# Copying a table of relative biases 128 times: out of SBUF, or from DRAM to DRAM

## The chip, the core and the metric

The kernel runs on one core of a Trainium2 chip. Its engines are TensorE (PE in the rows, its weight loads PEld), VectorE (DVE), ScalarE (ACT), GpSimd (POOL) and SyncE (SP). Here every transfer is issued by SP, in one queue, and carried by the core's 16 DMA engines. The metric is the device time of one execution in microseconds; before the change it is 3177.89 us, the median of three runs (3168.99, 3177.89 and 3178.84).

## The reference, cut to what matters

The reference is one inference step of a decoder layer, for 512 prompt tokens and 8 x 8 sample tokens that share all weights: a projection into four mixers (gated delta rule, a diagonal state space model S5, sliding-window attention with dilations, a gated linear recurrence), their product with `w_out`, cross attention, and a SwiGLU with a convolution. The change touches one input of the window attention, the T5 bias that each logit gets by its distance:

```python
for win, dil in DILATED:
    dist = jnp.arange(win // dil + 1, dtype=jnp.int32) * dil
    bias = rel_bias[t5_bucket(dist)].T.astype(jnp.float32)
    groups.append((dist, bias))
...
logits = jnp.einsum('bqhd,bqshd->bhqs', qi32, kg) * scale + bias[None, :, None, :]
```

`rel_bias` has 32 buckets by 8 heads. The kernel joins the three groups by a logarithm of how often a distance occurs, so that one table of 8 heads by 647 distances serves all of them.

## The kernel before, in words

All 576 tokens stay on chip, with features on partitions. A product with a weight matrix (`linear`, L132 on) takes the weights in blocks of 4 x 128 rows by 256 columns: `block` (L114 on) loads one of 512 KB into `raw` (L119, two buffers), ScalarE makes its upper part `hi` (L128, four instructions), VectorE its lower part `lo` (L129, four instructions), and TensorE does 48 matmuls (L151) with them into two PSUM tiles `acc`. A block's `raw` buffer is free for the block after next once its last `lo` is done, and after four blocks VectorE takes the sums out of `acc` (L1052 to L1054 in `conv4`), before TensorE may start on the next group.

A planner that simulates the engines writes the order of instructions for each engine, by priorities: weights first, then the work of the mixers, then the projections' matmuls as filling. It also shares out SBUF: a pool that is closed gives its place to a later one, and whoever first writes there waits for the last reader of what lay there. In `run`, the pool `st` of `swa_tables` is closed just before the pool `sm` of the S5 stage is opened on the same side.

`swa_tables` (L658 on) is the place of the change. It loads the one-hot table of buckets and the logarithms (`lm`, 8 partitions by 647), multiplies `rel` by the one-hots (L673) and adds the product to `lm` (L674). Then L675 writes `lm` to `rb` in DRAM, 8 heads by 128 copies by 647: each head's row 128 times. With the copies, a read whose partition step is 646 instead of 647 gives every query the table shifted by one place; `sample_new` (L891, L892, from 453 us of the profile on) and `swa_prompt` (L782, from 903 us on) read `rb` in this way.

Names of the rows that follow: `dn` is the delta rule's rows on their way to DRAM (L1251), `W` (L1736) and `u` (L1740) are what the S5 stage loads first into the pool `sm`, `hbg` (L1860) and `H` (L1763) are tiles of that pool which VectorE writes first, `hs` (L1766) and `rt` (L1751) are later loads of the stage, `ut` (L1742) is a copy of `u` that TensorE turns (L1745), and `old` (L813) are cached keys.

Of the kernel before, what the change touches and what calls it, by code (L numbers as in the profile page):

```python
# [7 lines left out]
F32 = mybir.dt.float32  # L8
# [4 lines left out]
PSUM = bass.MemoryType.PSUM  # L13
DRAM = bass.MemoryType.DRAM
NT = 576
EPS = 1e-6


class Net:
# [11 lines left out]
    @contextmanager  # L31
    def at(self, level, banks=None):
        """What is issued inside has this priority, and takes its PSUM banks in turn from these."""
        tc = self.tc
        saved, tc.cur_priority = tc.cur_priority, self.levels[level]
        old = self.banks
        self.banks = banks or old
        yield
        self.banks = old
        self.levels[level] = max(self.levels[level], tc.cur_priority)  # L40
        tc.cur_priority = saved
# [7 lines left out]
    def nt(self, n=NT, dtype=F32):  # L49
        """A row of all tokens, from a ring."""  # L50
        self.turn += 1
        return self.wo.tile([128, 604], dtype, name="nt", tag="m" + "hl"[self.turn % 2], bufs=6)[:, :n]

    def open(self):
        """What the first norm needs."""
        nc, cp, a = self.nc, self.cp, self.a
        self.ident = cp.tile([128, 128], F32, name="ident")
        self.gmix = cp.tile([128, 16], F32, name="gmix")
        with self.at("first", (3,)), self.tc.tile_pool(name="gp", bufs=1) as gp:
            nc.sync.dma_start(self.ident, a["c_ident"])  # L60
            g = gp.tile([16, 128], F32, name="g")
            nc.sync.dma_start(g, a["g_mix"][0].rearrange("(k p) -> k p", p=128))
            p = self.pm()
            nc.tensor.transpose(p[:, :16], g, self.ident[:16, :16])
            nc.scalar.copy(self.gmix, p[:, :16])

    def consts(self, vp):
        """Rows of 128 features each, turned into columns."""
# [30 lines left out]
    def rstd(self, pool, ss, n, scale, rows=128, eps=EPS, bufs=1):  # L99
        """1/sqrt(ss*scale + EPS) for ss [rows, n], with one Newton step."""  # L100
# [13 lines left out]
    def block(self, w, k0, nk, c0, ncol, gain=None):  # L114
        """nk row tiles by ncol columns of w, times the rows' gain if there is one, split into two parts of 12 bits."""
# [16 lines left out]
    def linear(self, xh, xl, w, c0, ncol, done, k0=0, nk=None, gain=None):  # L132
        """done(i, ps) gets each tile of 128 columns of x @ w as [128, 576]."""
# [24 lines left out]
    def project(self, c0, ncol, done):  # L158
        """Columns of the normed x @ w_in, but for 1/rms."""
        self.linear(self.xh, self.xl, self.a["w_in"][0], c0, ncol, done, gain=self.gmix)  # L160

    def mem_kv(self, mp, ahead):
        """Keys (turned) and values of the prompt's memory: out, and to DRAM for the cross attention."""
# [6 lines left out]
        for kb in range(0, 16, 2):  # L170
            if kb == 14:
                ahead()
            with self.at("drain"):
                # each row's scale waits for the products
# [47 lines left out]
    def first_x(self, fp, keep):  # L222
        """x turned, in two parts; 1/rms of each token, on every partition, joins the products."""
# [52 lines left out]
    def scaled(self, dst, ps, s=None):  # L276
        """A product's tile by the tokens' 1/rms."""
# [7 lines left out]
class Post(Net):  # L285
    def add_x(self, g=None, first=False):
        """What adds tiles of a product to x; after the last one x is scaled and split, and its squares summed."""
# [25 lines left out]
    def row_rstd(self):  # L313
        """1/rms of each token of xT, on every partition."""
# [28 lines left out]
    def sample_kT(self, cw, pair):  # L343
        """The cached memory's keys turned, two heads of each batch."""
# [11 lines left out]
    def cross(self, cw):  # L356
        """Two heads at a time; the product with w_mem_o takes the first two while the others are worked on."""
# [5 lines left out]
        def softmax(L, n):  # L363
            """rows of L [128, n, 256], in PSUM."""
# [31 lines left out]
        def sample(pair):  # L396
# [11 lines left out]
            # rows (j, b, t) in quarters; of a quarter's four batches each takes 128 columns  # L408
# [20 lines left out]
        def head(h, ps):  # L429
            q[h] = self.wo.tile([128, 604], F32, name="q", tag="ml", bufs=6)[:, :NT]  # L430
            nc.vector.tensor_tensor(q[h], ps, self.r, op=OP.mult)
            # block b of the mask's diagonal
# [27 lines left out]
    def ffn(self):  # L460
# [9 lines left out]
        with ExitStack() as c:  # L470
# [3 lines left out]
            with self.at("mix"):  # L474
                # rows (g, b, k): an eighth of the features each
# [15 lines left out]
            def states(ready):  # L491
                """These conv states, which are complete, out."""
# [9 lines left out]
            def conv(ft, ps, slot):  # L502
                """The taps of feature tile ft; its last raw rows go to the state."""
# [56 lines left out]
    def final(self, fh, fl, fw, fo):  # L560
        """The last part of the product with w_down by rows of tokens, x turned into the same sums; norm; out."""
# [14 lines left out]
        def turn(t):  # L576
            """x of a tile of tokens, by rows."""
# [45 lines left out]
def swa_consts():  # L623
    """One-hot buckets and logs of multiplicities by distance, and index masks: all by shapes alone."""
# [24 lines left out]
    # from (h, t) to the rows (hp, b2, h2, t), for each b2  # L649
# [7 lines left out]
class Swa(Post):  # L657
    def swa_tables(self, pool, sp):  # L658
        """Bias plus log multiplicity by distance, to DRAM 128 times: row p of a table starts p places earlier."""
# [15 lines left out]
        nc.sync.dma_start(self.rb, lm[:, None, :].to_broadcast([8, 128, ND]))  # L675
# [6 lines left out]
    def swa_open(self, sw):  # L682
        """What the projections leave for the sample; the prompt's q, k, v wait in DRAM."""
# [67 lines left out]
    def softmax_rows(self, pool, S, rows):  # L751
        """exp(S - max) over its sum, in place."""
# [8 lines left out]
    def swa_prompt(self, pool):  # L761
        nc = self.nc
        for hp in range(4):
# [4 lines left out]
            for j in range(2):  # L768
                h = 2 * hp + j
                r = slice(64 * j, 64 * j + 64)  # L770
                # both parts of q over one another, by either part of k twice
# [11 lines left out]
                for i in range(4):  # L783
# [5 lines left out]
                    # minus the logits, and minus their maximum  # L789
# [18 lines left out]
    def old(self, pool, name, k, t0):  # L808
        """Rows of one query each: row 16 * i + t of the cache's first 1536, i = 16 * k + i16 on partition (b, i16)."""
# [10 lines left out]
    def old_keys(self, t0):  # L820
        """Logits of the old keys of one query of each of the sample's batches."""
# [9 lines left out]
    def old_weights(self):  # L831
        """Exponentials of the old logits less their maximum; minus that, and their sum, by row."""
# [32 lines left out]
    def old_values(self, t0):  # L865
        """The values of one query of each batch, by their weights."""
# [11 lines left out]
    def sample_new(self):  # L878
        """Logits of the sample's queries with its new keys, and the biases of the cache's last 512 rows."""
# [27 lines left out]
    def sample_keys(self, pr, hp):  # L907
        """Logits of two batches' and two heads' queries with the cache's last 512 rows."""
# [18 lines left out]
    def sample_values(self, pr):  # L927
        """Two batches' weights, the old rows' joined by their maximum and sum, and the values by them."""
# [42 lines left out]
        # the new keys are done with: the outputs take their place  # L971
        nc.vector.tensor_copy(self.kTs[:, :, 16 * pr:16 * pr + 16], p[:, :64].rearrange("p (a b) -> p a b", a=4))

    def sample_out(self):
        """The old rows' values join by their weights."""
# [8 lines left out]
        for t0 in range(8):  # L984
            acc = pool.tile([128, 512], F32, name="oa", tag="kn", bufs=4)
            nc.sync.dma_start(acc, self.od[t0])
            # rows (t0, b)
# [17 lines left out]
def delta_consts():  # L1005
# [6 lines left out]
    for s in (b8, np.ones((128, 128), bool)):  # L1012
        # cumulative sums; c >= s, from s to c; s < c, from c to s
# [7 lines left out]
class Mix(Swa):  # L1021
    def conv_open(self, pool, cp):
        """The conv states with features on partitions, and where the new ones collect."""
# [20 lines left out]
    def conv4(self, ps, st, co, taps, bias=None):  # L1044
        """Four causal taps; each batch of the sample has its three states in front: [128, 600]; with a bias, the tokens alone."""
# [26 lines left out]
    def softplus(self, pool, x, rows, n):  # L1072
        """log(1 + exp(x)) = max(x, 0) + log1p(e), e = exp(-|x|); log1p(e) = 2 artanh(e / (2 + e))."""
# [17 lines left out]
    def out_rows(self, pool, co, nr, ntile, dests):  # L1091
        """co [128, ntile, nr] to rows of features; dests(g) gives (rows, address) of 512 columns."""
# [27 lines left out]
    def lru(self, pool, cv, then):  # L1120
        """Mixer D, tile by tile of its 512 channels."""
# [64 lines left out]
    def gelu2(self, x, u):  # L1186
        """2 gelu(x), by its tanh form."""
# [8 lines left out]
    def delta_ba(self, pool, cv):  # L1196
        """Beta and the decays' logarithms, by token."""
        nc, a = self.nc, self.a
        # b and a: both parts of their 8 columns at once
# [38 lines left out]
    def delta_proj(self, pool, cv):  # L1238
        """q, k, v (conv and twice silu) to DRAM; squares of q and k summed; the gates."""
# [15 lines left out]
    def delta_z(self, cv, then):  # L1255
        """z, twice silu, to DRAM; the conv states out."""
# [15 lines left out]
    def delta(self, pool):  # L1272
        nc, tc, a, o = self.nc, self.tc, self.a, self.o
        # the sample's masks go first; then the prompt's take their place
# [8 lines left out]
        # sums of g along each chunk, and over it for the sample  # L1283
# [22 lines left out]
        for i in (4, 0, 1, 2, 3):  # L1306
# [38 lines left out]
            # decays  # L1345
# [20 lines left out]
            # products of keys with keys and queries  # L1366
# [18 lines left out]
            # inverse of 1 + M: (1 - D)(1 + D^2)(1 + D^4) for its blocks of 8, then twice as wide at each level  # L1385
# [115 lines left out]
    def delta_out(self, pool):  # L1501
        """Norm and gate of the outputs."""
# [18 lines left out]
class S5(Mix):  # L1521
    def cmul(self, pool, shape, out, x, y, eng=None, tags=None):
        """out = x * y, each a pair (re, im)."""
# [12 lines left out]
    def s5_params(self, keep, pool):  # L1536
        """What depends on weights alone: R, its products with C and C's powers, to DRAM. Partitions are (g2, n), g = 2 gp + g2."""
# [25 lines left out]
        # th less its nearest multiple of 2 pi, in three parts; sine and cosine by the half angle  # L1563
# [16 lines left out]
        # the phase of eight steps  # L1580
# [18 lines left out]
        # (ab - 1) / a  # L1599
# [28 lines left out]
        # R[., gp, s, ch] = L^(7 - s) bb, eight pairs of groups at a time  # L1628
# [31 lines left out]
        # the skip joins lag 0, on the last 16 partitions  # L1660
# [18 lines left out]
        # C L^(t + 1), (re, -im) over partitions (ri, n)  # L1679
# [9 lines left out]
        with self.at("side"):  # L1689
# [5 lines left out]
            for j in (1, 2, 4, 8, 16, 32):  # L1695
                # phases j + 1 .. 2 j, as far as they are asked for
# [7 lines left out]
    def s5_proj(self, cv):  # L1704
        """u by token to DRAM."""
# [21 lines left out]
    def s5(self, pool):  # L1727
# [5 lines left out]
        # phases and magnitudes by chunk  # L1733
# [13 lines left out]
        # sums over each chunk  # L1747
# [12 lines left out]
        # states at the chunks' starts, at 0 .. 63 and 65 .. 72; the prompt's last at 64  # L1760
# [9 lines left out]
        # the prompt's turned back by each chunk's phase: then a real scan by the magnitude  # L1770
# [23 lines left out]
        # the sample's, one step  # L1794
# [76 lines left out]
class Full(S5):  # L1871
    def w_load(self, group):
        """A mixer's output in two parts."""
# [12 lines left out]
    def w_out(self, group, g=None, parts=None, first=False):  # L1886
        """A mixer's part of the product with w_out joins x."""
# [4 lines left out]
    def keep_x(self, k):  # L1892
        """A row of x with its features on partitions to DRAM."""
# [4 lines left out]
    def sample_step(self, i):  # L1898
        """The sample's attention, spread over the projections' tiles."""
# [131 lines left out]
```

## Time and profile before

| | |
|---|---|
| median of three runs | 3177.89 us (3168.99 to 3178.84) |
| span of the profiled execution | 3171.8 us |
| TensorE matmuls | 3015.4 us busy, 95% |
| VectorE | 1712.5 us busy, 54% |
| ScalarE | 962.5 us busy, 30% |
| 16 DMA engines, SP's queue | 364.82 MB, 37.5% busy |

The profiled execution's span is the time from its first to its last instruction. What lies around it is not on the page; the span itself lies between the lowest and the median of the three timed runs. In the page's strips the span is cut into 40 slices of 79.3 us, and a digit is the busy share in tenths. A granted clock of 1.00 is TensorE's upper level of 2.4 GHz, 0.50 the lower of 1.2 GHz.

### The profile page before, as it was taken

The page shows a single profiled execution, that of the slowest core. Times are in us where ns is not written, and L with a number is a line of the kernel's source. Part 1 is how long each engine was busy: PE and PEld are TensorE (multiplying, and loading weights), DVE is VectorE, ACT ScalarE, POOL GpSimd, SP SyncE. Part 2 cuts the span into 40 slices and gives each one's busy share as a digit, 9 for nine tenths or more (in the row PEclk, how much of TensorE's full clock was granted, in tenths as well). Part 3 has the DMA queues.
Part 4 walks back from the last instruction along what each step waited for, and adds up shares of the span by engine and source line. Part 5 has one row for each costly group of instructions (what it writes and reads, how often), then busy time and mean ns, then how long its engine had stood idle before and what let it go on. Part 6 is the DMA issues. An engine that isn't in the chain of part 4 may idle for free.

```text
span 3171.8 us, 53645 instructions
## 1 busy us (share of the span) xinstructions
PE 3015.4 (95%) x22323; PEld 2868.6 (90%) x22323; DVE 1712.5 (54%) x2878; ACT 962.5 (30%) x1612; POOL 434.7 (14%) x563
## 2 busy tenths in 40 slices
PE   8948998999989999999999999999999999999998
PEld 8847897787878879979999999999999999999997
DVE  7827756678667575557444444443434444444354
ACT  4413331343423353324322222221222222222233
POOL 4102233213212001203010101010100000000000
PEclk9979999999999999999999999999999999999999
DMA  5454566535566464232222222222222222222232
GB/s 163 139 107 133 154 190 201 161 115 176 171 201 190 142 214 139 87 109 67 82 87 81 86 82 82 87 81 87 81 86 83 81 88 80 88 81 83 85 121 74
DMA packets 350572, 368.26 MB, mean 116 GB/s; under 512 B 35838, under 2 KB 298708, under 8 KB 349625
## 3 DMA queue, kind: packets, MB, share of 16 engines
q1 hardware_dynamic: 350328, 364.82, 37.5%
q8 instruction: 176, 2.88, 0.4%
q14 instruction: 68, 0.55, 0.1%
HBM read 317.79 MB, written 46.97 MB: 115 GB/s over the span
## 4 chain that ended last, share of the span: by engine, by line
PE 80%; DMA 7%; DVE 7%; issue 2%; SPq 2%; ACT 1%; another core or an unknown queue 1%; POOL 1%; DVEq 0%; ACTq 0%; POOLq 0%
PE acc L151 69%; PE acc L602 2%; DVE lo L129 1%; DMA old<-in_cache_win_k 1%; PE pm L1393 1%; PE pm L924 1%; PE acc L194 1%; DMA kn<-in_cache_win_k 1%; SPq L119 1%; DMA old<-in_cache_win_v 1%; PE pm L803 1%; DMA raw<-in_w_down 1%; DMA dw<-dn 0%; DVE acc L875 0%
## 5 line engine op out<-in xcount | busy, mean ns | idle before, releaser
L151 PE MATMUL acc<-xh,hi 128*128 128x288 f32 x4224 | 922.9, 299 | 60.5 <-DVE dco L1054 41.0
L151 PE MATMUL acc<-xl,hi 128*128 128x288 f32 x4224 | 925.1, 299 | 3.0 <-DVE xl L245 3.0
L151 PE MATMUL acc<-xh,lo 128*128 128x288 f32 x4224 | 914.5, 299 | 1.2 <-DVE lo L129 1.2
L151 PEld LDWEIGHTS acc<-xh,hi 128*128 128x128 f32 x4224 | 687.0, 190 | 73.2 <-issue 67.5
L124 DVE TENSOR_TENSOR lo<-raw,hi 128x1024 fp32r<-128x1024 f32 x322 | 397.1, 1233 | 593.3 <-ACT hi L123 580.7
L151 PEld LDWEIGHTS acc<-xl,hi 128*128 128x128 f32 x4224 | 688.7, 190 | 11.4 <-issue 7.1
L151 PEld LDWEIGHTS acc<-xh,lo 128*128 128x128 f32 x4224 | 685.3, 190 | 8.3 <-issue 5.2
L123 ACT CAST hi<-raw 128x1024 fp32r<-128x1024 f32 x322 | 337.9, 1049 | 1090.8 <-PE acc L151 1001.1
L151 PE MATMUL acc<-mh,hi 128*128 128x288 f32 x1920 | 420.7, 299 | 8.5 <-DVE xT L303 7.1
L151 PE MATMUL acc<-mh,lo 128*128 128x288 f32 x1920 | 416.0, 296 | 0.2 <-DVE lo L124 0.2
L151 PE MATMUL acc<-ml,hi 128*128 128x288 f32 x1920 | 415.6, 296 | 0.0
L303 DVE TENSOR_TENSOR xT<-acc,xT 128x576 f32<-128x576 f32 x240 | 181.3, 756 | 274.3 <-PE acc L151 273.7
L151 PEld LDWEIGHTS acc<-mh,hi 128*128 128x128 f32 x1920 | 307.6, 189 | 17.5 <-DVE xT L303 8.7
L151 PEld LDWEIGHTS acc<-ml,hi 128*128 128x128 f32 x1920 | 309.2, 189 | 3.9 <-issue 3.2
L151 PEld LDWEIGHTS acc<-mh,lo 128*128 128x128 f32 x1920 | 308.5, 188 | 3.5 <-issue 2.9
L515 POOL COPY co<-ub 128x2 f32<-128x2 f32 x88 | 61.1, 694 | 1290.3 <-DVE ub L507 1290.3
L128 ACT ACTIVATE hi<-raw,gmix 128x256 fp32r<-128x256 f32 x320 | 136.6, 498 | 260.1 <-PE acc L151 172.4
L129 DVE SCALAR_TENSOR_TENSOR lo<-raw,gmix,hi 128x256 fp32r<-128x256 f32 x320 | 168.9, 573 | 47.8 <-ACT hi L128 47.4
L523 DVE SCALAR_TENSOR_TENSOR y<-ub,vec,y 128x592 f32<-128x592 f32 x176 | 146.4, 832 | 42.7 <-ACT y L521 40.3
L521 ACT ACTIVATE y<-ub,vec 128x592 f32<-128x592 f32 x88 | 69.7, 792 | 158.1 <-DVE ub L508 156.2
L507 DVE TENSOR_TENSOR ub<-acc,sq 128x512 f32<-128x512 f32 x88 | 60.6, 688 | 54.0 <-PE acc L151 54.0
L1393 PE MATMUL pm<-dw 128*128 128x128 f32 (+1 forms) x456 | 61.3, 280 | 7.6 <-DVE dw L1407 4.2
(645 smaller groups left out, 2771.5 us busy)
## 6 DMA issues: line engine op xcount, KB each, us to landing
raw<-in_w_up SPq DMA_DIRECT2D x176, 512.0 KB
raw<-in_w_down SPq DMA_DIRECT2D x88, 512.0 KB
raw<-in_w_in SPq DMA_DIRECT2D x80, 512.0 KB
raw<-in_w_out SPq DMA_DIRECT2D x32, 512.0 KB
old<-in_cache_win_k SPq DMA_DIRECT2D x48, 256.0 KB
old<-in_cache_win_v SPq DMA_DIRECT2D x48, 256.0 KB
kn<-in_cache_win_k SPq DMA_DIRECT2D x32, 256.0 KB
v<-in_cache_win_v SPq DMA_DIRECT2D x32, 256.0 KB
```

The costliest lines, as they stand in the source:

```text
L123: nc.scalar.copy(hi, raw)
L124: nc.vector.tensor_tensor(lo, raw, hi, op=OP.subtract)
L128: nc.scalar.activation(hi[:, k], raw[:, k], AF.Copy, scale=g)
L129: nc.vector.scalar_tensor_tensor(lo[:, k], raw[:, k], g, hi[:, k], op0=OP.mult, op1=OP.subtract)
L151: nc.tensor.matmul(acc[m][:, 224 + 288 * j:512 + 288 * j], wt[:, k, 128 * m:128 * m + 128], at(x, kb + k)[:, 288 * j:288 * j + 288], start ...
L303: nc.vector.tensor_tensor(x, ps, old, op=OP.add)
L507: nc.vector.tensor_tensor(u[:, 2:514], ps[:, :512], self.r[:, :512], op=OP.mult)
L515: nc.gpsimd.tensor_copy(co[:, 0:2, ft % 4], u[:, 512:514])
L521: nc.scalar.activation(y, u[:, :592], AF.Copy, scale=w(0))
L523: nc.vector.scalar_tensor_tensor(y, u[:, k:k + 592], w(k), y, op0=OP.mult, op1=OP.add)
L602: nc.tensor.matmul(ps, x[k][:, tok], z[:, k, cs], start=k == 0 and i == 0, stop=k == 3 and i == 2)
L1393: nc.tensor.matmul(p[:n, n * h:n * h + n], lhs[:, h], rhs[:, h], start=True, stop=True)
```

## The change

The table `lm` goes to a new DRAM tile `row` of 8 by 647 first, once. A second transfer then writes `rb` from `row`, both ends in DRAM. The rest of the difference is comments that were left out, with no effect.

```diff
-        nc.sync.dma_start(self.rb, lm[:, None, :].to_broadcast([8, 128, ND]))
+        row = self.dp.tile([8, ND], F32, name="rb1")
+        nc.sync.dma_start(row, lm)
+        nc.sync.dma_start(self.rb, row[:, None, :].to_broadcast([8, 128, ND]))
```

Line numbers behind it move by two. The planner orders what follows anew. On SP's queue, around the table's transfers, this stood before (the loads named `raw` are weight blocks):

```order
L119 DMA raw<-in_w_in 128x4x256
L1251 DMA dn<-nt 128x576
L675 DMA rb<-lm 1024x1x647
L1251 DMA dn<-nt 128x576
L119 DMA raw<-in_w_in 128x4x256 x2
L1736 DMA W_3301<-wt 128x1024
L1736 DMA W_3302<-wt 128x1024
L1740 DMA u_3305<-us 72x8x128
L1740 DMA u_3323<-us 72x8x128
L1766 DMA hs<-in_state_ssm_re 128x128
L119 DMA raw<-in_w_in 128x4x256
```

And this now, where `rb_1616` is the new tile `row`:

```order
L119 DMA raw<-in_w_in 128x4x256
L1253 DMA dn<-nt 128x576
L676 DMA rb_1616<-lm 8x647
L677 DMA rb<-rb_1616 1024x1x647
L1253 DMA dn<-nt 128x576
L119 DMA raw<-in_w_in 128x4x256
L1738 DMA W_3303<-wt 128x1024
L1738 DMA W_3304<-wt 128x1024
L1742 DMA u_3307<-us 72x8x128
L1742 DMA u_3325<-us 72x8x128
L1768 DMA hs<-in_state_ssm_re 128x128
L119 DMA raw<-in_w_in 128x4x256 x2
```

One of the two weight loads behind `dn` has moved behind the five loads of the S5 stage. On VectorE, between the table's last addition (L674) and the next sums taken out of `acc`, this stood before:

```order
L674 TENSOR_TENSOR lm<-pm,lm 8x135
L1049 MEMSET nt 128x3
L1050 COPY nt<-dst 128x8x3
L1248 SCALAR_TENSOR_TENSOR nt<-nt 128x512
L1250 SCALAR_TENSOR_TENSOR nt<-nt 128x64
L129 SCALAR_TENSOR_TENSOR lo<-raw,gmix,hi 128x256 x4
L680 COPY po<-pm 128x48
L129 SCALAR_TENSOR_TENSOR lo<-raw,gmix,hi 128x256 x4
L1763 MEMSET H 128x32
L1860 TENSOR_SCALAR hbg<-vec 128x4
L129 SCALAR_TENSOR_TENSOR lo<-raw,gmix,hi 128x256 x4
L1052 TENSOR_TENSOR nt<-acc,rB 128x512
```

And this now:

```order
L674 TENSOR_TENSOR lm<-pm,lm 8x135
L1051 MEMSET nt 128x3
L1052 COPY nt<-dst 128x8x3
L1250 SCALAR_TENSOR_TENSOR nt<-nt 128x512
L1252 SCALAR_TENSOR_TENSOR nt<-nt 128x64
L129 SCALAR_TENSOR_TENSOR lo<-raw,gmix,hi 128x256 x4
L1765 MEMSET H 128x32
L1862 TENSOR_SCALAR hbg<-vec 128x4
L682 COPY po<-pm 128x48
L129 SCALAR_TENSOR_TENSOR lo<-raw,gmix,hi 128x256 x8
L1054 TENSOR_TENSOR nt<-acc,rB 128x512
```

The two first writes into the pool `sm` stand one weight block earlier. From here to the end of the S5 stage neighbouring instructions change places on all engines, mostly by a few positions; before and behind that stretch the orders are the same, but for one swap of two short VectorE instructions far behind.

## Rows read from the trace of the kernel before

**Rows 1.** The page: span; matmuls' busy share, granted clock and DMA share in 40 slices.
```profile
span 3171.8 us, 53645 instructions
...
PE   8948998999989999999999999999999999999998
...
PEclk9979999999999999999999999999999999999999
DMA  5454566535566464232222222222222222222232
```

**Rows 2.** Windows: stretch, length, busy time (count) by engine, granted clock, DMA share, GB/s.
```profile
158.00:193.00 35.00, 33.80 (x247) 31.93 (x245) 16.09 (x41) 9.86 (x20) 0.00 (x0) 1.00 0.51 104
193.00:234.00 41.00, 0.10 (x1) 0.13 (x1) 3.10 (x10) 1.91 (x5) 0.72 (x2) 0.55 0.58 102
234.00:250.00 16.00, 12.44 (x68) 11.95 (x69) 8.63 (x20) 7.09 (x14) 2.12 (x3) 0.66 0.62 155
250.00:317.00 67.00, 55.19 (x494) 52.90 (x493) 52.35 (x91) 22.83 (x50) 19.45 (x14) 0.95 0.44 132
1350.00:3171.00 1821.00, 1798.88 (x13312) 1771.74 (x13310) 826.53 (x1097) 476.22 (x608) 144.75 (x285) 1.00 0.27 85
```

**Rows 3.** Waits, 160 to 262 us: us in total, times, longest.
```profile
ACT hi L128 <- DMA raw<-in_w_in: 49.1, 1, 49.1
DVE hbg L1860 <- DMA rb<-lm: 46.4, 1, 46.4
...
PE acc L151 <- DVE dco L1054: 41.0, 1, 41.0
```

**Rows 4.** Timeline of SP's queue: start, duration of the issue, line, transfer, count.
```profile
166.01 0.39 SPq L119 DMA_DIRECT2D raw<-in_w_in  x1
168.15 0.35 SPq L1251 DMA_DIRECT2D dn<-nt  x1
172.45 0.78 SPq L675 DMA_DIRECT2D rb<-lm  x1
173.33 19.47 SPq L1251 DMA_DIRECT2D dn<-nt  x1
192.90 17.62 SPq L119 DMA_DIRECT2D raw<-in_w_in  x2
228.10 0.90 SPq L1736 DMA_DIRECT2D W<-wt  x2
```

**Rows 5.** Waits of SP's queue, 166 to 240 us.
```profile
SPq L1736 <- DMA rb<-lm: 17.5, 1, 17.5
```

**Rows 6.** Timeline, 160 to 262 us, VectorE: the last `lo` of the two ready blocks.
```profile
175.18 1.68 DVE L129 SCALAR_TENSOR_TENSOR lo<-raw,gmix,hi 128x256 fp32r<-128x256 f32 x4 [1.93 <-ACT hi L128]
...
180.52 1.69 DVE L129 SCALAR_TENSOR_TENSOR lo<-raw,gmix,hi 128x256 fp32r<-128x256 f32 x4 [2.83 <-ACT hi L128]
```

**Rows 7.** Timeline, 226 to 242 us: the next block, until TensorE goes on.
```profile
228.60 0.48 DVE L1860 TENSOR_SCALAR hbg<-vec 128x4 f32<-128x4 f32 x1 [46.39 <-DMA rb<-lm]
...
230.80 1.70 ACT L128 ACTIVATE hi<-raw,gmix 128x256 fp32r<-128x256 f32 x4 [49.11 <-DMA raw<-in_w_in]
231.34 1.68 DVE L129 SCALAR_TENSOR_TENSOR lo<-raw,gmix,hi 128x256 fp32r<-128x256 f32 x4 [2.27 <-ACT hi L128]
...
233.90 0.82 PE L151 MATMUL acc<-xh,hi 128*128 128x288 f32 x2 [40.95 <-DVE dco L1054]
```

**Rows 8.** Chain that ended last: start, us, what.
```profile
163.49 2.03 DMA hot<-in_c_hot
...
228.03 0.02 issue
...
436.58 3.69 DMA mixT<-gth
```

**Rows 9.** Transfers, KB each; then packets and engines' share, 176 to 190 us.
```profile
rb<-lm SPq DMA_DIRECT2D x1, 2588.0 KB
...
u<-us SPq DMA_DIRECT2D x4, 288.0 KB
W<-wt SPq DMA_DIRECT2D x2, 512.0 KB
...
hs<-in_state_ssm_re SPq DMA_DIRECT2D x1, 64.0 KB
...
DMA packets 270, 0.70 MB, mean 50 GB/s; under 512 B 0, under 2 KB 0, under 8 KB 270
...
q1 hardware_dynamic: 270, 0.70, 46.8%
```

**Rows 10.** Windows as in rows 2: cached keys (`old`), then a store of `dn`.
```profile
503.00:510.00 7.00, 7.00 (x62) 6.77 (x61) 2.46 (x5) 2.08 (x5) 0.94 (x1) 1.00 0.52 168
...
168.50:170.00 1.50, 1.50 (x13) 1.50 (x12) 1.43 (x3) 0.00 (x0) 0.00 (x0) 1.00 0.85 313
```

**Rows 11.** SP's queue again: what ran in the first of those windows.
```profile
500.85 10.13 SPq L813 DMA_DIRECT2D old<-in_cache_win_k  x6
```

## The prediction

> **What bounds the kernel now.** I read the page's strips first. Matmuls keep TensorE 0.9 or more busy nearly everywhere, except in the third slice, whose digit is 4; there the granted clock falls to 0.7 while the DMA engines are 0.5 busy [rows 1]. Windows around this slice say more: from 193 to 234 us TensorE works 0.10 of 41 us, VectorE 3.10 and ScalarE 1.91 [rows 2]. All of them wait. From 1350 us to the end TensorE is busy 1798.88 of 1821 us [rows 2], so a microsecond that is given back early has nothing later to disappear in.
>
> The waits name two things that end almost together. VectorE stood 46.4 us at `hbg` for the transfer that writes `rb`, since `hbg` lies where `lm` lay and that transfer still read it. ScalarE stood 49.1 us for a weight block, and TensorE 41.0 us for the sums that VectorE had not taken out of `acc` [rows 3]. SP's queue shows why the weights were late. `rb` is issued at 172.45; the small store behind it takes 19.47 us to issue, so the next two weight blocks are issued only from 192.90, and that takes 17.62 us [rows 4]. Yet their buffers were free at 176.9 and 182.2, when the two blocks' `lo` ended [rows 6]. So the queue was full of `rb`. Then SP waits 17.5 us more for `rb` [rows 5], which has landed at 228.03 [rows 8], and the loads of the S5 stage follow. Each cause alone would have held TensorE nearly as long.
>
> **The transfer removed.** 2588 KB are 2.650 MB. From 176 to 190 us only its packets run: 270 packets, 50 GB/s, 46.8% of 16 engines, which is 7.5 engines [rows 9]. At 50 GB/s the data take 53.0 us; from issue to landing (172.45 to 228.03) are 55.6, so 2.6 us are fixed. A packet of 2588 bytes holds its engine 0.468 x 16 x 14 / 270 = 0.39 us.
>
> **The store added.** `lm` to DRAM is 20 KB. SP waits until it has landed before it issues the copy. No row shows such a store; a small load of the same step (`hot`) takes 2.03 us, a store of 288 KB 3.69 us [rows 8]. I take 2.0, since size is what the second has more of. Behind the wait stand the store of `dn`, for which nobody hurries here, and the next weight block, whose buffer is free at 176.9 anyway, so the wait itself costs nothing but that it delays the copy to 174.5.
>
> `hbg` and `H` now stand before the second block's `lo`, and wait for this store alone instead of the 46.4 us. It lands near 174.5, before VectorE gets there, at 176.9 [rows 6]. Were it late by 2 us, the idle 2.83 us before the second `lo` cover it. The second weight block moves behind `W` twice, `u` twice and `hs`, 1.70 MB [rows 9]: 5.4 us at the fastest rate of the rows, 313 GB/s [rows 10], 11 at the 155 of 234 to 250 us [rows 2]. The block before it hides 48 matmuls of 33.80 / 247 = 0.137 us [rows 2], 6.6 us. I cost the move at nothing; with the slow rate it would be 4 us, less what `u` gains by it.
>
> **The copy added.** How fast DRAM to DRAM goes, no row shows; all other transfers have one end in SBUF. The nearest row is that of `old`, which reads 8 sequences out of DRAM: an outer dimension of 8, as the new source has. While six of them run, the engines are 0.52 busy, that is about 8 of 16, and move 168 GB/s [rows 10, 11]. At that rate the copy takes 2.650 / 0.168 = 15.8 us. The fast end is a store of `dn` on all engines, 313 GB/s [rows 10]: 8.5 us. The slow end is the old rate, 53.0 us: nothing in the rows tells whether 50 GB/s come from the 8 source partitions or from writing 1024 rows of 2588 bytes to DRAM. I take 15.8, because a store to DRAM at 313 GB/s and a load out of it at 168 on half the engines both run several times faster than 50, so the reading of 8 partitions is what is special about the old transfer.
>
> The Trainium skill bears on this in two places. SBUF — State Buffer, Door 1: The DMA port swizzle, says that a transfer's rate depends on how many of 16 ports its partitions reach; partitions 0 to 7 lie on two, for some 54 GB/s as an estimate from the page's 27.2 per port. The trace's 50 GB/s agrees. By that rule the limit leaves with the source. The Trainium skill's DMA: Bandwidth & Descriptors, Rules for kernel authors, speaks against a full gain: an outer dimension below 16 confines a transfer to that many engines, and the source still has 8 heads outermost. By this the copy doesn't reach the 8.5 us of all engines, and the sum stays at 37 instead of 45 us. The same page of the Trainium skill, Latency and other measured facts, gives copies between HBM tensors 207 GB/s on all engines; half of this, an estimate, is 104 GB/s or 25.6 us, and the sum would be 27.
>
> **The sum.** Issue 174.5, fixed 2.6, data 15.8: landed at 192.9 instead of 228.03. The next weight block follows right behind it in the queue, as before. Before, 2.8 us after the landing ScalarE had the block (230.80), and TensorE went on at 233.90, 5.9 us after the landing, behind `lo` and the sums out of `acc` [rows 7]. The same 5.9 us give 198.8 now. TensorE's two ready blocks last until 193.0, as before. The stall shrinks from 41 to 6 us, a gain of 233.9 - 198.8 = 35.1 us.
>
> To this comes the clock. From 234 to 250 us it stood at 0.66, on its lower level (1.2 GHz) most of the time, after TensorE had been idle for 41 us; TensorE worked 12.44 of these 16 us [rows 2]. At the upper level this work takes 8.2 us, so at most 4.2 are to be had. The matmuls there also wait for `u`, so I take half, 2 us. Sum: 37 us. From 250 to 317 us TensorE works 55.19 and VectorE 52.35 of 67 [rows 2]. That stretch hangs on the chain of the S5 stage, which starts from `W` and `u` and moves ahead as a whole. The new order there may win or lose some of TensorE's 11.8 idle us; I take nothing for it and half of them, 6 us, as noise either way.
>
> The profiled execution's span of 3171.8 us would become 3134.8. It is 6.1 us below the median of the runs, 3177.89; with the same 37 us off, the median becomes 3141.
>
> **Rivals.** *Half the rate.* Each byte is now read from and written to the same DRAM. For it: no row shows both ends there, and the 16 readers and writers of one memory may share what loads or stores have alone. Against: 313 and 168 GB/s leave room for 336 in both directions. At 84 GB/s the copy takes 31.5 us, lands at 208.6, TensorE goes on at 214.5: 19 us gained, 1 from the clock, 3158.
>
> *It stays as slow.* The 7.5 busy engines are the limit, not the partitions; the new source has the same 8 rows, so 53.0 us remain. VectorE is freed at 176.9, but TensorE then waits for the weight block, which lies behind the copy in the queue. The copy lands 2 us later than before, at 230.1; 3180, no change. For it: the two waits end together, so that removing one is worth nothing. Against: `old` on as many engines is 3.4 times as fast.
>
> *Slower than before.* Each of the 8 rows is read 128 times from one place, and rows of 2588 bytes start at uneven places in DRAM, now at both ends. If packets queue there, the copy is slower than out of SBUF; from 50.9 us on (52 GB/s) each further microsecond is lost one for one, since the weight block waits behind it. At 33 GB/s it takes 80 us, lands at 257 and TensorE goes on at 263: 29 us lost, 3207. Against: nothing else reads at this time, and the loads in the rows are nowhere so slow.
>
> *All engines.* If the copy is spread over 16 engines, 8.5 us, it lands at 185.6 and the weight block is ready before 193.0. The stall is gone: 41 and 4 us, 3133.
>
> **How the numbers follow.** The forecast (copy of 13 to 20 us, gain of 30 to 45 us with the noise of the order) has a chance of 0.58, its own range is 3131 to 3148. Half the rate (20 to 40 us) has 0.20, as slow 0.09, slower 0.08, all engines 0.05. A range of 3128 to 3164 holds the first, four fifths of the second and most of the last, some 0.79. A measurement of this kernel tells a change from none from about 0.3%, 9.5 us. Faster by more: 0.58 + 0.20 + 0.05 = 0.83; within: 0.09; slower: 0.08.
>
> **What would show it.** In the profile of the changed kernel, SP's wait for the small store should be 2 us; the copy alone in the queue should show about 8 busy engines and some 165 GB/s; `hbg` should have no wait on `rb`; TensorE's stall near 193 us should be about 6 us and end with a weight block, no longer with `rb`; and the clock there should keep its upper level nearly throughout. The prediction is wrong if the copy takes more than 25 us, if TensorE stands at 193 us for anything other than the block behind the copy, or if the S5 stage, from 250 to 317 us before, becomes longer by more than 6 us in its new order.

## The result and the profile after

The changed kernel takes 3131.03 us, the median of four runs (3129.54 to 3137.14), against 3175.61 us for four runs of the kernel before, three of which are those of the table above. The medians differ by 44.6 us. The ratio on record is 0.9869, with a 95% interval of 0.9851 to 0.9886: 1.1 to 1.5% faster. A second set of runs gave 0.9864 (0.9846 to 0.9881). The prediction was 3141 us, a gain of 37 us; 3131.03 lies at the lower edge of the forecast's own range, 3131 to 3148.

The page of the profiled execution (3129.54 us, span 3127.7): span; matmuls' busy share, granted clock and DMA share in 40 slices.

```profile
span 3127.7 us, 53649 instructions
...
PE   8998989999999999989999999999999999999998
...
PEclk9999999999999999999999999999999999999999
DMA  5455566545575553322222222222222222222232
```

The 4 in the third slice and the 7 of the clock under it [rows 1] are gone. The stretch of the stall, as in [rows 2]: stretch, length, busy time (count) of PE, PEld, DVE, ACT and POOL, granted clock, DMA share, GB/s.

```profile
193.00:234.00 41.00, 36.00 (x351) 34.99 (x352) 30.14 (x53) 18.66 (x41) 11.69 (x10) 0.92 0.56 167
```

From 193 to 234 us TensorE now works 36.00 of 41 us instead of 0.10. What follows now runs some 43 us earlier, so later windows of the two profiles don't hold the same work. SP's queue, which answers to [rows 4]: start, duration of the issue, line, transfer, count. L676 is the small store into `row` (the trace names it `rb`, too), L677 the copy.

```profile
171.56 0.29 SPq L676 DMA_DIRECT2D rb<-lm  x1
173.10 0.73 SPq L677 DMA_DIRECT2D rb<-rb  x1
173.93 5.52 SPq L1253 DMA_DIRECT2D dn<-nt  x1
179.54 1.06 SPq L119 DMA_DIRECT2D raw<-in_w_in  x1
180.70 4.38 SPq L1738 DMA_DIRECT2D W<-wt  x2
185.13 4.91 SPq L1742 DMA_DIRECT2D u<-us  x2
190.09 3.25 SPq L1768 DMA_DIRECT2D hs<-in_state_ssm_re  x1
193.44 3.16 SPq L119 DMA_DIRECT2D raw<-in_w_in  x2
```

Behind the copy, the store of `dn` takes 5.52 us to issue instead of 19.47, and the weight block goes out at 179.54 instead of 192.90. Waits of SP, then of the engines from 160 to 262 us (total, times, longest), for [rows 3]:

```profile
SPq L677 <- DMA rb<-lm: 1.2, 1, 1.2
```

```profile
ACT hi L128 <- DMA raw<-in_w_in: 13.5, 2, 12.8
...
PE acc L151 <- DVE dco L1056: 4.6, 1, 4.6
...
DVE hbg L1862 <- PE pm L680: 0.7, 1, 0.7
```

`hbg` no longer waits for a transfer. The timeline of the next block until TensorE goes on, for [rows 7]:

```profile
193.56 1.70 ACT L128 ACTIVATE hi<-raw,gmix 128x256 fp32r<-128x256 f32 x4 [12.76 <-DMA raw<-in_w_in]
194.10 1.68 DVE L129 SCALAR_TENSOR_TENSOR lo<-raw,gmix,hi 128x256 fp32r<-128x256 f32 x4 [12.78 <-ACT hi L128]
...
196.66 0.82 PE L151 MATMUL acc<-xh,hi 128*128 128x288 f32 x2 [4.60 <-DVE dco L1056]
```

TensorE stands 4.60 us where it stood 40.95, and goes on 3.10 us after ScalarE has the block, to the hundredth as before. Packets of the copy alone, 176 to 180 us (count, MB, share of 16 engines):

```profile
DMA packets 254, 0.66 MB, mean 164 GB/s; under 512 B 0, under 2 KB 0, under 8 KB 254
...
q1 hardware_dynamic: 254, 0.66, 49.1%
```

That is 7.9 engines and 0.12 us a packet (0.491 x 16 x 4 / 254), where it was 0.39.

### The profile page after: what moved, and what is told of

The parts are those of the page before. It is cut to its first block, busy times and chain, and to the rows that moved or that the text cites. A ratio compares the mean times of both kernels' runs of the same rounds, so it can differ in the third digit from the quotient of the medians.

```text
span 3127.7 us, 53649 instructions
## 1 busy us (share of the span) xinstructions
PE 3010.8 (96%) x22323; PEld 2867.6 (92%) x22323; DVE 1715.1 (55%) x2878; ACT 962.6 (31%) x1612; POOL 437.0 (14%) x563
## 4 chain that ended last, share of the span: by engine, by line
PE 80%; DVE 8%; DMA 7%; issue 2%; ACT 1%; SPq 1%; POOL 1%; DVEq 0%; ACTq 0%; POOLq 0%
PE acc L151 68%; PE acc L602 2%; DVE lo L129 2%; DMA old<-in_cache_win_k 1%; PE acc L194 1%; PE pm L1395 1%; DMA od<-acc 1%; PE pm L926 1%; DMA kn<-in_cache_win_k 1%; DVE acc L877 1%; DMA raw<-in_w_down 1%; DMA old<-in_cache_win_v 1%; PE pm L805 1%; DMA dw<-dn 0%; DMA raw<-in_w_in 0%
```

## The experiments

The theory: the old transfer is slow because it reads 8 neighbouring partitions, and what holds TensorE is this transfer's time. It holds by two ways at once, so that opening one gives nothing: `hbg` and `H` wait for its place (A), and the weight blocks wait behind it (B). The rivals say that one of the two ways, or the new order, was the gain. Every ratio below is to the kernel before, with its 95% interval.

### Opening the two ways, with the transfer as slow as before

**Place, first try.** `lm` in a pool of its own, closed after the S5 stage.

```diff
-        lm = sp.tile([8, ND], F32, name="lm")
+        lm = self.lk.tile([8, ND], F32, name="lm")
...
```

> The table goes out of its 8 SBUF partitions as before the change, in SP's queue; only its place in SBUF is now kept until the S5 stage is over, so that hbg and H wait for no transfer. Theory (the slow transfer fills the queue and the weight blocks lie behind it): hbg and H run near 177 us, yet the next weight block still arrives behind the 53 us of the transfer, TensorE still stands about 41 us near 193 and ends with a weight block; 3170 to 3180 us, no gain. Rival A (the gain came from freeing the place early): TensorE goes on near 197 as after the change, some 3131 to 3138 us. Rival B (the planner's new order brought it): the order here is close to the one after the change in that hbg and H stand where their inputs allow, so a gain would be seen here too.

Measured: 1.0006 (0.9993 to 1.0019). Waits, 160 to 262 us:

```profile
DVE nlam L1112 <- DMA rb<-lm: 45.5, 1, 45.5
...
PE acc L151 <- DVE lo L129: 38.0, 1, 38.0
```

The edit only moved the wait: the pool that came to lie there next has its first write (`nlam`) early in VectorE's order, and VectorE stood there instead. The time is the expected one, but this run doesn't tell A from B.

**Queue.** The same transfer, issued by ScalarE.

```diff
-        nc.sync.dma_start(self.rb, lm[:, None, :].to_broadcast([8, 128, ND]))
+        nc.scalar.dma_start(self.rb, lm[:, None, :].to_broadcast([8, 128, ND]))
```

> The same slow transfer out of 8 SBUF partitions, with lm's place shared as before, but issued on ScalarE's queue, so that nothing lies behind it in SP's. Theory (two waits in parallel, each of them enough to hold TensorE): the weight blocks arrive by 193 us, but hbg or H on VectorE still waits for the transfer, some 50 us, and the sums out of acc behind it; TensorE stands about 38 to 41 us; 3165 to 3180 us, little or no gain. Rival A (only the place counts) gives the same here, so it is told from the theory by the run before. Rival D (only the queue counts): the stall is gone or short, 3128 to 3140 us.

Measured: 0.9989 (0.9978 to 1.0000). Waits:

```profile
DVE hbg L1860 <- DMA rb<-lm: 46.8, 1, 46.8
...
PE acc L151 <- DVE dco L1054: 39.0, 1, 39.0
...
ACT hi L128 <- DMA raw<-in_w_in: 24.1, 1, 24.1
```

As expected, `hbg` still holds TensorE. But the weight blocks did not come by 193 us: ScalarE waits 24.1 us for one, although the slow transfer is no longer in SP's queue.

**Both edits.**

> Both edits together: the slow transfer out of 8 SBUF partitions stands on ScalarE's queue and lm's place is kept. It still takes 53 us or more and shares the 16 DMA engines with the weight blocks. Theory: with both waits gone the stall is gone or nearly (0 to 6 us) although the transfer is as slow as ever, apart from what the blocks lose by sharing 7 to 8 of the engines; 3126 to 3140 us. If the slow transfer's rate alone were what counts (its load on the engines, not the waits), the blocks would still be late and the time stays above 3155 us.

Measured: 0.9991 (0.9979 to 1.0003), 3172.35 us, where 3126 to 3140 were expected; `nlam` waited 46.6 us and TensorE 39.0. It fails as a test for the same reason as the first.

**Place, second try.** `lm` shares its place with `vns`, which VectorE first writes at 557 us (the expectation's 900 us is wrong, with no effect here).

```diff
-        lm = sp.tile([8, ND], F32, name="lm")
+        lm = self.lk.tile([8, ND], F32, name="lm", tag="vn")
...
-        self.vns = sw.tile([64, 512], F32, name="vns")
+        self.vns = sw.tile([64, ND], F32, name="vns", tag="vn")[:, :512]
...
```

> The first run on the place only moved the wait: the next pool to lie there (nlam, lwa of the linear recurrence) waited for rb in place of hbg. Here lm shares its place with a tile that is first written after 900 us, so nothing waits for it; the slow transfer stays on SP's queue. Theory: hbg, H and nlam run without a wait on rb, ScalarE still waits for a weight block until about 230 us, and TensorE stands about 41 us; 3168 to 3180 us, no gain. Rival A (place): stall under 10 us, 3128 to 3140 us.

Measured: 0.9972 (0.9958 to 0.9986), 3167.9 us. Waits:

```profile
ACT hi L128 <- DMA raw<-in_w_in: 49.4, 1, 49.4
...
PE pm L1745 <- ACT ut L1742: 44.4, 2, 43.9
...
DVE hbg L1860 <- PE pm L678: 0.7, 1, 0.7
```

Now nothing waits for the place, `hbg` runs at 176.70 as after the change, and TensorE stands as long as ever; what it waits for is now `u`, which is issued behind the slow transfer as the block is. Rival A falls. So does the new order as the main cause: `hbg` and `H` stand before the second block's `lo` here, too, and SP's queue has one block, `W`, `u`, `hs` and then two blocks, as after the change. The 9 us that this kernel did gain (4 to 13) are more than the theory gave. Of the 6.6 us between the spans of the two profiles, 2.0 are shorter waits of TensorE for VectorE in the S5 stage (8.7 us for 10.7); I found no row that accounts for the rest.

**Both, with the place of the second try.**

> As the run before it, with the slow transfer on ScalarE's queue as well: neither the place nor SP's queue holds anything back. What is left is that the transfer's packets (0.38 us each) still occupy 7 to 8 of the 16 engines for 53 us, and with the transfer on its own queue alone the weight block came only at 205.5 us. Theory, so amended: hbg has no wait on rb, the block comes at about 205, the stall is 12 to 17 us; 3143 to 3158 us: most of the gain but not all. If either wait alone were the cause, this would be no better than one of the single edits; if the engines' sharing costs nothing, the stall is under 5 us and the time 3128 to 3136 us.

Measured: 0.9968 (0.9952 to 0.9985), 3166.49 us, where 3143 to 3158 were expected. Waits, then SP's queue, then the packets from 210 to 222 us (q10 is ScalarE's queue, q1 SP's):

```profile
PE pm L1745 <- ACT ut L1742: 37.6, 1, 37.6
...
ACT hi L128 <- DMA raw<-in_w_in: 24.2, 1, 24.2
```

```profile
187.16 14.76 SPq L1740 DMA_DIRECT2D u<-us  x2
201.97 19.33 SPq L1766 DMA_DIRECT2D hs<-in_state_ssm_re  x1
```

```profile
DMA packets 456, 0.80 MB, mean 67 GB/s; under 512 B 9, under 2 KB 200, under 8 KB 456
...
q10 hardware_dynamic: 229, 0.59, 45.8%
q1 hardware_dynamic: 227, 0.21, 5.0%
```

The block came at 206.41, as the amended theory said; but then TensorE's next work in order was to turn `ut`, for which `u` was still on its way. SP's queue is choked although the slow transfer isn't in it: its loads move 0.21 MB in 12 us, while ScalarE's queue holds 7.3 of 16 engines. So B is not a matter of the queue alone. Nor are the loads' packets slower beside the transfer: 0.21 MB at 5.0% of 16 engines in 12 us are 22 GB/s for each busy engine. Here is SP's queue in the kernel before from 230 to 233 us, when the transfer has landed, with 23 GB/s for each busy engine:

```profile
q1 hardware_dynamic: 461, 1.07, 96.2%
```

So the loads' packets are about as fast as ever while they run; fewer of them come to run. That some of each load's packets have to wait behind those of the slow transfer on the engines that it holds is my reading; no row tells on which engine a packet ran. The Trainium skill, DMA: Bandwidth & Descriptors, Issuing engines are not separate DMA queues, says that transfers of all issuing engines run on the same 16 engines, and that another issuer saves only the time of issuing. This run and the first on ScalarE's queue agree: ScalarE waited 24.2 and 24.1 us for the block.

### Changing the transfer's time

**Source partitions apart.** The 8 rows on partitions 0, 4, ... 28, both ways left closed.

```diff
+        rw = sp.tile([32, 32], F32, name="rw")
+        nc.gpsimd.memset(rw, 0.0)
+        nc.gpsimd.tensor_copy(rw.rearrange("p (h f) -> p h f", f=4)[:, :, 0], rel)
...
-            nc.tensor.matmul(p[:8, :n], rel, hot[:, c0:c0 + n], start=True, stop=True)
+            nc.tensor.matmul(p[:32, :n], rw, hot[:, c0:c0 + n], start=True, stop=True)
...
-        nc.sync.dma_start(self.rb, lm[:, None, :].to_broadcast([8, 128, ND]))
+        nc.sync.dma_start(self.rb, lm[0:32:4][:, None, :].to_broadcast([8, 128, ND]))
```

> The transfer stays out of SBUF, with 8 rows of the same size read 128 times, one transfer in SP's queue as before and lm's place shared; but the 8 rows lie on partitions 0, 4, ... 28 instead of 0 to 7, with the table spread by a product of 32 columns. Theory (what is slow is reading 8 neighbouring partitions): packets become as short as in the copy from DRAM, about 0.1 us instead of 0.39, the transfer takes 14 to 18 us, hbg waits for it until about 191 us, the stall is 4 to 8 us; 3128 to 3140 us. Rival E (any read of SBUF by few partitions, or the writing of 1024 rows, is slow; DRAM as a source is what helps): packets stay at 0.39 us and the time at 3170 to 3182 us. In between, with packets near 0.2 us: stall 18 to 25 us, 3145 to 3160 us.

Measured: 0.9870 (0.9851 to 0.9890), 3135.24 us. Packets, 174 to 177 us, and TensorE's three waits near 193 us:

```profile
DMA packets 234, 0.62 MB, mean 206 GB/s; under 512 B 0, under 2 KB 0, under 8 KB 233
...
q1 hardware_dynamic: 233, 0.60, 51.8%
```

```profile
193.26 0.49 PE L151 MATMUL acc<-xh,hi 128*128 128x288 f32 x2 [0.75 <-DVE dco L1058]
...
197.69 0.47 PE L1749 MATMUL pm<-ident,ut 72*128 72x72 f32 x4 [2.35 <-ACT ut L1746]
...
199.61 1.22 PE L1749 MATMUL pm<-ident,ut 72*128 72x72 f32 x8 [1.45 <-ACT ut L1746]
```

The gain of the change without DRAM as the source: some 8 engines, as before, move 206 GB/s instead of 50, and `hbg` waits 7.2 us. VectorE and SP's queue have the old order here (`hbg` and `H` behind the second block's `lo`, two blocks before `W`), so the gain doesn't need the new one.

**Half as far apart.** The edit of the run above, with `[32, 16]`, `f=2` and `lm[0:16:2]`: partitions 0, 2, ... 14.

> As the run with the 8 rows on partitions 0, 4, ... 28, but on partitions 0, 2, ... 14. Theory (packets are slow in proportion to how close the source partitions lie): a step of 1 gave 0.39 us a packet, a step of 4 gave 0.11; a step of 2 gives 0.19 to 0.22, the transfer takes 27 to 30 us and lands near 201, hbg waits for it until then, the stall is 13 to 17 us and the time 3142 to 3152 us. Rival G (any gap between the partitions is enough): 0.11 us, 3129 to 3136 us as there. Rival H (a step of 2 doesn't help): 0.39 us and 3168 to 3180 us.

Measured: 0.9915 (0.9900 to 0.9930), 3148.32 us, `hbg` waited 20.0 us. Packets, 176 to 182 us, and TensorE:

```profile
DMA packets 232, 0.60 MB, mean 100 GB/s; under 512 B 0, under 2 KB 0, under 8 KB 232
...
q1 hardware_dynamic: 232, 0.60, 48.5%
```

```profile
207.40 0.82 PE L151 MATMUL acc<-xh,hi 128*128 128x288 f32 x2 [14.04 <-DVE dco L1058]
```

With rows 1, 2 and 4 partitions apart the rate is 50, 100 and 206 GB/s on as many engines, and the time follows. The Trainium skill, SBUF — State Buffer, Door 1: The DMA port swizzle, puts these rows on 2, 4 and 8 ports; at the page's 27.2 GB/s a port, an estimate of 54, 109 and 218. The trace agrees: the measured rates lie 5 to 8% below.

**The copy made twice**, the second one into a tile that nobody reads.

```diff
+        rb2 = self.dp.tile([8, 128, ND], F32, name="rb2")
+        nc.sync.dma_start(rb2, row[:, None, :].to_broadcast([8, 128, ND]))
```

> The changed kernel with the copy made twice, the second time into a DRAM tile that nobody reads. Theory (weight blocks lie behind the copy, the stall follows its time one for one): 15.8 us more on the same 8 engines, the first weight block lands near 206, TensorE goes on near 212.5 instead of 196.7; with some 2 to 6 us more for the low clock and the fill-up behind a longer stall, 3146 to 3154 us. Rival (the length of the copy doesn't matter, only that hbg no longer waits for it): 3129 to 3136 us, as the changed kernel.

Measured: 0.9915 (0.9899 to 0.9930), 3148.58 us.

```profile
209.94 0.85 PE L151 MATMUL acc<-xh,hi 128*128 128x288 f32 x2 [17.49 <-ACT hi L128]
```

Beside the changed kernel's run on the same chip (3130.51 us, a stall of 5.3 us, below) the stall is 12.2 us longer and the time 18.1 us; `hbg` had no wait on the copy here either. So the copy's length counts, even where the place is free.

**All engines.** The copies outermost instead of the heads.

```diff
-        nc.sync.dma_start(self.rb, row[:, None, :].to_broadcast([8, 128, ND]))
+        nc.sync.dma_start(self.rb.rearrange("h c d -> c h d"), row[None, :, :].to_broadcast([128, 8, ND]))
```

> The changed kernel, with the copy's 128 copies as the outer dimension instead of the 8 heads. Theory (8 outer rows use 8 engines; the stall shrinks one for one with the transfer's time): 16 engines busy instead of 8, about 330 GB/s, the data take 8 to 9 us instead of 15.8; the next weight block is there before 193 us, the stall of 4.6 us is gone and with it part of the low clock behind it (0.72 to 0.82 from 193 to 208 us, worth some 3 us); 3120 to 3127 us, 0.1 to 0.3% under the changed kernel. Rival F (both ends in one memory: 168 GB/s are its limit): 16 engines with packets of some 0.21 us, still 15.8 us, 3128 to 3134 us, as the changed kernel.

Measured: 0.9851 (0.9833 to 0.9870), 3129.13 us. Packets, 178 to 186 us, and TensorE:

```profile
DMA packets 700, 1.82 MB, mean 227 GB/s; under 512 B 0, under 2 KB 0, under 8 KB 699
...
q1 hardware_dynamic: 699, 1.81, 104.9%
```

```profile
194.65 0.50 PE L151 MATMUL acc<-xh,hi 128*128 128x288 f32 x2 [1.75 <-DVE dco L1056]
```

All 16 engines are busy, but a packet now takes 0.19 us (1.049 x 16 x 8 / 699) instead of 0.12: 227 GB/s, neither the theory's 330 nor rival F's 168. The stall shrinks from 4.60 to 1.75 us. That the kernel gained by it is not shown; the intervals overlap.

**128 rows.** The table on 128 partitions, 16 for each head, each written 8 times; no copy from DRAM.

```diff
+        rw = sp.tile([32, 8, 16], F32, name="rw")
+        nc.gpsimd.tensor_copy(rw, rel.unsqueeze(2).to_broadcast([32, 8, 16]))
...
-        nc.sync.dma_start(self.rb, lm[:, None, :].to_broadcast([8, 128, ND]))
+        nc.sync.dma_start(self.rb.rearrange("h (q c) d -> (h q) c d", q=16), lm[:, None, :].to_broadcast([128, 8, ND]))
```

> No copy from DRAM: the table is computed on 128 partitions (16 per head), each of which is written 8 times, one transfer from SBUF to DRAM; hbg and H wait for it, since lm's place is shared as before. Theory (a transfer out of SBUF is slow only when few neighbouring partitions are read): 313 GB/s as for the store of dn, 8 to 9 us, so hbg waits until about 183 us instead of 176.6; the blocks behind it arrive before 193, no stall or one under 3 us; 3118 to 3130 us. Rival E' (writing 1024 rows of 2588 bytes to one place is slow from SBUF): packets near 0.39 us on 16 engines, 25 us, stall about 15 us, 3140 to 3148 us.

Measured: 0.9837 (0.9818 to 0.9856), 3126.77 us. From 175 to 181 us:

```profile
DMA packets 748, 1.95 MB, mean 325 GB/s; under 512 B 0, under 2 KB 0, under 8 KB 747
```

TensorE's only waits near 193 us are 1.4 us for `ut`. To see whether it beats the change, both ran again on one chip.

> The changed kernel once more, beside the others on the same chip: 3128 to 3137 us as before.

> The table computed on 128 partitions and written 8 times from each, once more, beside the changed kernel on the same chip. Theory (no stall is left near 193 us, the clock stays at its upper level): 4 to 10 us under the changed kernel, 3118 to 3129 us. If the first run's advantage was chance, the two agree within 3 us.

Measured: 0.9864 (0.9846 to 0.9881), 3130.51 us, for the changed kernel, and 0.9860 (0.9841 to 0.9879), 3130.71 us, for the 128 rows. In these two profiles the waits near 193 us differ by 4.7 us (5.31 and 0.46 against 1.09), and TensorE's waits for `acc` to be emptied in the S5 stage take 1.9 us back (10.4 with the 128 rows, 8.5 in the changed kernel). What is left is too little for these runs to tell; the first run's advantage is not shown.

### Waits and times together

TensorE's waits near 193 us, for sums out of `acc`, for a block or for `ut`, with the times:

| kernel | waits, us | ratio |
|---|---|---|
| before | 40.95 + 3.56 | 1 |
| place, first try | 38.0 + 3.6 | 1.0006 |
| place, second try | 43.9 + 0.5 | 0.9972 |
| other queue | 39.0 + 2.6 | 0.9989 |
| both, first try | 39.0 | 0.9991 |
| both, second try | 37.6 | 0.9968 |
| copy twice | 17.5 | 0.9915 |
| 2 apart | 14.0 + 3.6 | 0.9915 |
| 4 apart | 0.75 + 3.8 | 0.9870 |
| changed kernel, two profiles | 4.6; 5.3 + 0.5 | 0.9869; 0.9864 |
| all engines | 1.75 | 0.9851 |
| 128 rows, two profiles | 1.4; 1.1 | 0.9837; 0.9860 |

40 us less of waiting (44.5 to 4.6) go with 42 us less time (1.3% of 3176), and 27 us less, in two different ways, with 27 (0.85%). Two rows stray from this line by 9 us, the second try on the place and the first run of the 128 rows; the others by less than 5.

## Why the prediction was right, and where 7 us were missing

**The copy** ran as taken: 164 GB/s for 168, on 7.9 engines. The reason given for 15.8 us, that 8 neighbouring partitions are special, is shown by the steps of 1, 2 and 4. The rivals with half the rate, the old rate and less did not occur; that of all engines could not have had its 8.5 us from DRAM, since 16 engines move 227 GB/s there, which makes 11.7. In this copy, half the engines have 72% of the rate of all. The 207 GB/s of the Trainium skill (DMA: Bandwidth & Descriptors, Latency and other measured facts), which the page gives for tiles whose rows lie 512 KiB apart, are near the 227; the half that the prediction took of them for 8 engines, 104 (25.6 us), is far from the measured 164.

**The store** made SP wait 1.2 us instead of 2.0. The table was done 0.9 us sooner (171.56 for 172.45), and the copy was issued at 173.10 instead of 174.5. ScalarE had the block at 193.56, where the prediction's landing and its 2.8 us gave 195.7.

**The stall** became 4.6 us for 6, a gain of 36.4 for 35.1.

**The clock** was to give 2 us, and to keep its upper level nearly throughout. **`u`** was to give nothing, and that is the step that failed: "I cost the move at nothing; with the slow rate it would be 4 us, less what `u` gains by it." Here is the stretch from TensorE's return to the end of 56 matmuls for `acc` and 24 that turn `ut`, of the kernel before and then of the changed one (columns as above):

```profile
233.90:251.60 17.70, 14.13 (x80) 13.64 (x81) 9.94 (x24) 8.07 (x16) 2.12 (x3) 0.69 0.60 152
```

```profile
196.66:208.70 12.04, 12.04 (x80) 12.01 (x81) 9.27 (x22) 7.75 (x15) 2.27 (x3) 0.74 0.76 206
```

The same 80 matmuls take 5.66 us less: 2.09 us less busy time (14.13 - 12.04), and 3.57 us of idle time, all of it gone. The busy time is the clock's. Pieces of the same stretches, before and then after:

```profile
233.90:237.50 3.60, 3.60 (x14) 3.35 (x14) 1.76 (x3) 0.69 (x1) 0.00 (x0) 0.50 1.03 195
238.00:241.00 3.00, 0.40 (x4) 0.32 (x4) 0.00 (x0) 0.65 (x2) 0.62 (x2) 1.00 0.31 89
241.60:248.10 6.50, 6.46 (x31) 6.47 (x32) 6.03 (x16) 4.42 (x9) 0.91 (x2) 0.50 0.64 176
```

```profile
196.66:202.60 5.94, 5.94 (x30) 5.91 (x31) 3.21 (x5) 3.74 (x8) 1.22 (x2) 0.50 0.83 226
```

Before, TensorE came back at the lower level for 3.6 us, and worked at it for another 6.5 us behind the wait for `ut`. After the change it came back at the lower level all the same, for 5.9 us, although it had stood for 4.6 us instead of 41. So the clock did not keep its upper level, and what was gained is that TensorE works through one such stretch instead of two: 4.2 us less at half the speed are 2.1 us. That this meets the predicted 2 is luck. Whether the second stretch went because the wait for `ut` went, no run shows by itself. The prediction's bound was too low as well: its 0.66 averages in the wait, in which the granted clock stood at 1.00; 10.1 us of work at the lower level left 5 us to be had, not 4.2.

The idle time was the wait for `ut`:

```profile
240.60 0.47 PE L1745 MATMUL pm<-ident,ut 72*128 72x72 f32 x4 [3.00 <-ACT ut L1742]
...
241.63 1.22 PE L1745 MATMUL pm<-ident,ut 72*128 72x72 f32 x8 [0.56 <-ACT ut L1742]
```

The second weight block moved behind `W`, `u` and `hs`; so `u` is there in time, and the block is not late. The gain from `u` is 3.6 us where nothing was put. The runs with rows 2 and 4 apart kept the old order of these loads (two blocks, then `W` and `u`) and kept waits for `ut` of 3.6 and 3.8 us; with the copy made twice the new order stood, and this wait was absent.

**The sum**: 36.4 + 2.1 + 3.6, the 0.9 us before the stall, and 1.1 us over the rest make the 44.1 us between the two spans; predicted were 37. Of the 7 us that were missing, `u` is 3.6, the shorter stall 1.3, and what lies before and behind the stretch 2.0. Single runs of the changed kernel lie between 3129.54 and 3137.14 us, so that last part is within their scatter. The new order in the S5 stage, allowed 6 us either way, did little: TensorE's two longest waits there are 6.98 and 2.81 us before, 6.81 and 2.11 after.

**The two waits**: that each alone would have held TensorE nearly as long is shown for both. The prediction put the second down to the queue being full; with the transfer in another queue the loads were late all the same, which matters to whoever thinks of another queue as the cure. That would not have changed its sum.

## What to carry to other kernels

When engines stand still around a large transfer, open each way by which it holds them, one at a time, and look in the trace for the wait that takes over; here the place, the queue and both together were worth 0.3% at most, and only shortening the transfer gave the gain. The place from which a repeated transfer reads decided that time here: 8 neighbouring partitions were the slowest source, and DRAM, partitions 4 apart, or all 128 partitions each gave the whole gain, partitions 2 apart two thirds of it. Loads that reorder around such a transfer have a price of their own: look up who waits for each of them before it is costed at nothing. And a short stall is not free of the clock: here 4.6 us of standing were followed by 5.9 us at the lower level.

## What was not expected of the hardware

- 8 rows read from partitions 1, 2 and 4 apart: 50, 100 and 206 GB/s, with 7.5, 7.8 and 8.3 engines busy.
- A copy from DRAM to DRAM of rows of 2588 bytes: 164 GB/s on 8 engines, 227 on 16, with packets of 0.12 and 0.19 us.
- A transfer that keeps 7.3 engines busy out of another queue left SP's loads 0.21 MB in 12 us, while about half the engines stood idle (45.8 and 5.0% busy).
